# Weight block sums made in the units that use them, first-half operands prepared on a plan, three raw tiles for the second half's operands

## The chip, the cores and the metric

The kernel runs on one core of a Trainium2 chip. The metric is the device time of one execution in microseconds (us), lower is better. A profiled execution gives the trace; the other executions are timed without the profiler. The engines of a core are TensorE (PE: matmul, and PEld: its weight load), VectorE (DVE), ScalarE (ACT), GpSimd (POOL) and SyncE (SP), which here only issues DMAs. Each engine works through its own instructions in a fixed order.

## What is computed

One layer of a streaming encoder over 2048 frames of width 1024, in float32: a mixer of four groups, projected back and added to the input, and then a feed-forward network (FFN). The change touches the end of the mixer's output projection and the FFN:

```python
y = rmsnorm(y, group_norm[l].reshape(N_GROUPS, GROUP_W)).reshape(bsz, seq, D_MIX)
x = x + (y @ w_out[l]).astype(x.dtype)
h = rmsnorm(x, norm_ffn[l])
x = x + (jnp.square(jax.nn.relu(h @ w_ff1[l])) @ w_ff2[l]).astype(x.dtype)
```

`w_ff1` is 1024 x 4096, `w_ff2` is 4096 x 1024.

## The kernel before

**Precision.** Each float32 operand is split into a high part (ScalarE copies it to a rounded type, hi) and a low part (VectorE subtracts, lo = x - hi), and each product runs as three matmuls, hi·hi, hi·lo and lo·hi.

**The FFN products** are done in Winograd's form of Strassen's scheme: 2 x 2 blocks, seven block products in place of eight, with sums of blocks before and after. The time axis is cut in two halves `hf`, each of two blocks of 512 frames.

**Output projection.** `outp(b)` for the four blocks b of 512 frames: two column halves, four tiles each, 24 matmuls a tile (L510 to L512 in the trace); the result and the residual x are added (L1101) in a tile with tag `xr` and stored in `x1_d[b]`. `outp` yields 32 times, every 6 matmuls. `out_in(b)` makes the operand of the projection, in `hh` and `hl`, from the stored group outputs. `out_in(b + 1)` runs beside the second half of `outp(b)`; `dense(g, side)` lets the main generator `g` run, advances `side` at given steps, and `advance()` steps the generators that `track` has registered. After the loop over b = 0, 1, 2 the mixer's pools are closed, and `outp(3)` runs.

**Operands of the first FFN product.** `prep_step(hf, i, put, tmp)` takes 128 rows of the two time blocks of a half from `x1_d` (L1234, tiles with tag `xt`, two buffers), norms them (L1236 to L1238, gain in a tile with tag `gain`), transposes them on PE (L1228) and forms the seven operands, of which `put` splits each (L1267, L1268). Operands 5 and 6 lie in the buffers `hh` and `hl`, which the output projection reads until its last tile. For the first half the four steps are written behind `outp(3)` with a high priority; for the second half they run inside the first product at j = 2, 5, 8, 11, and the seven operands are kept in DRAM (`tb_d`). `from_dram` (L1286 to L1288) loads these in 14 pieces of 512 KB through the two `xt` buffers when the second half begins, and splits them.

**First product.** For each half and each j of 16, `w_units(j)` loads four blocks of `w_ff1` into the ring of raw tiles (tag `wr`, six buffers, L1204), forms four sums (L1208; two of them in tiles with tag `xr`, `tmpw`) and splits seven operands (L1198, L1199; nine buffers each of `wh`, `wl`). `ff1` then does seven products of 12 matmuls (`prod`, L1324), squares the ReLU (L1330, L1331), and stores seven operands for the second product in `as_d`.

**Second product.** Seven passes n, in the order AT = (0, 1, 6, 2, 3, 4, 5) of the block products; eight tiles q in each; 48 matmuls a tile (L1489). The tile of `as_d` is loaded through the two `xt` buffers and split (`s_tile`, L1457 to L1459). The weight operand of pass n and block row k is made by `t_unit(n, k)`: a raw tile of `w_ff2`, or of the sums in DRAM `tt_d`, split into one of 23 pairs of buffers (9 of `wh`/`wl`, 14 of `vh`/`vl`). The units of pass n + 1 are written in pass n, from q = 3 on, with a high priority.

**Sums for the second product.** `w2_step(n)`, 32 of them, loads pieces of the four blocks of a block row of `w_ff2` into one of two tiles named `w2r` (L1419), makes four sums with VectorE (L1208, 128 x 256) and stores them in `tt_d` (L1434). They are written into the second product's loop; the order that the framework's scheduler makes of it, which is fixed when the kernel is built, has them from within the first product on, wherever their buffers allow.

The framework sets the order of instructions on each engine, by priority and by when buffers come free; SyncE's DMA issues have such an order too, and an issue that waits holds up the ones behind it.

Of the kernel before, what the change touches and what calls it, by code (L numbers as in the profile page):

```python
# [21 lines left out]
P = 128  # L22
# [37 lines left out]
def emit(ctx, tc, a):  # L60
# [994 lines left out]
                yield  # L1055


    def out_in(b):
        yh, yl = hh, hl
        ya = c1.tile([P, 2, TB], F32, tag="gain", name="yat")  # L1060
        SY.dma_start(out=ya, in_=ya_d[b].rearrange("(c p) t -> p c t", p=P))

        def load(i):
            yt = big.tile([P, 3 * GW], F32, tag="xt", name="ybt", bufs=2)
            r0 = (b % 2) * TB + i * P
            SY.dma_start(out=yt[:, 0:GW], in_=yb_d[b // 2][r0:r0 + P, :])
            SY.dma_start(out=yt[:, GW:], in_=ycd_d[b][i * P:(i + 1) * P, :])
            return yt

        nx = load(0)  # L1070
        yield
        for i in range(4):
            ti = slice(i * P, (i + 1) * P)
            yt = nx
            if i < 3:
                nx = load(i + 1)
            S.activation(out=yh[:, 0:2, ti], in_=ya[:, :, ti], func=AF.Copy)
            V.tensor_tensor(out=yl[:, 0:2, ti], in0=ya[:, :, ti], in1=yh[:, 0:2, ti], op=ALU.subtract)
            for k3 in range(2):
                pt = psum_tr()  # L1080
                for k in range(3):
                    kk = k3 * 3 + k
                    PE.transpose(pt[:, k * P:(k + 1) * P], yt[:, kk * P:(kk + 1) * P], ident)
                pv = pt[:, 0:384].rearrange("p (k t) -> p k t", k=3)
                oh = yh[:, 2 + k3 * 3:5 + k3 * 3, ti]
                ol = yl[:, 2 + k3 * 3:5 + k3 * 3, ti]
                S.activation(out=oh, in_=pv, func=AF.Copy)
                V.tensor_tensor(out=ol, in0=pv, in1=oh, op=ALU.subtract)
                yield
# [80 lines left out]
    for b in range(3):  # L1170
        g = outp(b)
        for n in range(16):
            next(g)
            advance()
        drain(*((), ("s5",), ("hg",))[b])
        nxt = out_in(b + 1)
        next(nxt)
        dense(g, nxt)
        run(nxt)
    mixs.close()  # L1180


# [1 line left out]

    NJ = DFF // (2 * P)
    as_d = [[dram.tile([P, 4, NJ, P], F32, name=f"as{i}_{h}") for h in range(2)] for i in range(7)]
    tt_d = [dram.tile([NJ, P, D], F32, name=f"tt{i}") for i in range(2)]
    tb_d = [dram.tile([P, 4, TB], F32, name=f"tb{i}") for i in range(7)]
    run(outp(3))

    f2 = ExitStack()
    th = f2.enter_context(tc.tile_pool(name="th", bufs=1, reuse_waits="tile"))
    hi_ = tc.high_priority
# [17 lines left out]
    def operands():  # L1211
        ops = []
        for i in range(5):
            ops.append([th.tile([P, 4, TB], F32R, tag=f"t{i}{p_}", name="tb") for p_ in "hl"])
        for n_ in ("hh", "hl"):
            both = big.tile([P, KD, TB], F32R, tag=n_, name="tb2")
            ops.append([both[:, 0:4], both[:, 4:8]])
        return ops

    g_ffn = c1.tile([P, D], F32, tag="gain", name="g_ffn")  # L1220
    with hi_():
        SY.dma_start(out=g_ffn, in_=a["norm_ffn"].partition_broadcast(P))

    def prep_step(hf, i, put, tmp):
        def trans(ps, xs, half):
            for k in range(4):
                kk = half * 4 + k
                PE.transpose(ps[:, k * P:(k + 1) * P], xs[:, kk * P:(kk + 1) * P], ident)  # L1228

        o = i * P  # L1230
        xs = []
        for tb in range(2):
            x_ = big.tile([P, D], F32, tag="xt", name="fxs", bufs=2)
            SY.dma_start(out=x_, in_=x1_d[hf * 2 + tb][o:o + P, :])  # L1234
            ss = c1.tile([P, 1], F32, tag="fss", name="fss", bufs=2)
            S.activation(out=junk, in_=x_, func=AF.Square, accum_out=ss)  # L1236
            r = rstd_of(c1, ss, 1, 1.0 / D, "frs")
            V.scalar_tensor_tensor(out=x_, in0=x_, scalar=r, in1=g_ffn, op0=ALU.mult, op1=ALU.mult)  # L1238
            xs.append(x_)
        p11, p22 = psum_tr(), psum_sx()  # L1240
        trans(p11, xs[0], 0)
        trans(p22, xs[1], 1)
        s11, s22 = tmp(), tmp()
        S.activation(out=s11, in_=p11, func=AF.Copy)
        S.activation(out=s22, in_=p22, func=AF.Copy)
        p12, p21 = psum_tr(), psum_sx()
        trans(p12, xs[1], 0)
        trans(p21, xs[0], 1)
# [30 lines left out]

    def from_dram():  # L1280
        ops = operands()
        for i in range(7):
            for h in range(2):
                ks = slice(h * 2, h * 2 + 2)
                r = big.tile([P, 2, TB], F32, tag="xt", name="tr", bufs=2)
                SY.dma_start(out=r, in_=tb_d[i][:, ks, :])  # L1286
                S.activation(out=ops[i][0][:, ks], in_=r, func=AF.Copy)  # L1287
                V.tensor_tensor(out=ops[i][1][:, ks], in0=r, in1=ops[i][0][:, ks], op=ALU.subtract)  # L1288
        return ops
# [2 lines left out]
        return a["w_ff2"][(2 * k + half) * P:(2 * k + half + 1) * P, nd * 512:(nd + 1) * 512]  # L1292


    def w_units(j, tmp):
        f0 = j * 2 * P

        def raw(kh, fh):
            return raw512(a["w_ff1"][kh * 512:(kh + 1) * 512, f0 + fh * P:f0 + (fh + 1) * P]
                          .rearrange("(k p) c -> p k c", p=P))  # L1300

        with hi_():
            a11, a12, a21, a22 = raw(0, 0), raw(1, 0), raw(0, 1), raw(1, 1)
            u = [split(a11), split(a12)]
            s1, s2 = tmpw(), tmpw()
# [66 lines left out]
    def tmpw():  # L1372
        return c1.tile([P, 512], F32, tag="xr", name="tw", bufs=2)

    with hi_():
        b = operands()
        for i in range(4):
            prep_step(0, i, put_split(b), tmp1)
    nxt = w_units(0, tmp1)
    for hf in range(2):  # L1380
        for j in range(NJ):
            u = nxt
# [14 lines left out]
        return t2p.tile([P, 512], F32, tag="tq", name="tq", bufs=NT2)  # L1397

    units = [0]
    NB2 = 14  # L1400

    def split2(raw):
        n = units[0] % (NW + NB2)
        units[0] += 1
        return split(raw) if n < NW else split(raw, t2p, ("vh", "vl"), NB2)

    w2s = {}  # L1410

    def w2_load(n):
        k, c = n // 2, n % 2
        if n % 2:
            t_ = c1.tile([P, 4, 256], F32, tag="gain", name="w2r")
        else:
            t_ = t2p.tile([P, 4, 256], F32, tag="w2r", name="w2r")
        for h in range(2):
            SY.dma_start(out=t_[:, 2 * h:2 * h + 2, :], in_=a["w_ff2"][(2 * k + h) * P:(2 * k + h + 1) * P, :]  # L1419
                         .rearrange("p (d c) -> p d c", d=2)[:, :, c * 256:(c + 1) * 256])  # L1420
        w2s[n] = t_

    def w2_step(n):
        k, c = n // 2, n % 2
        if n + 1 < 2 * NJ:
            w2_load(n + 1)
        t_ = w2s.pop(n)
        b11, b12, b21, b22 = (t_[:, i, :] for i in range(4))
        tsub(b11, b12, b11)
        tsub(b12, b22, b12)  # L1430
        tsub(b22, b22, b11)
        tsub(b21, b21, b22)
        for h in range(2):
            SY.dma_start(out=tt_d[h][k].rearrange("p (d c) -> p d c", d=2)[:, :, c * 256:(c + 1) * 256],  # L1434
                         in_=t_[:, 2 * h:2 * h + 2, :])
# [4 lines left out]
    def t_unit(n, k):  # L1440
        i = AT[n]
        with hi_():
            if i in (0, 1, 6):
                return split2(raw512(w2(k, *((0, 0), (1, 0), None, None, None, None, (1, 1))[i])))
            h, c = ((1, 1), (0, 1), (1, 0), (0, 0))[i - 2]
            return split2(raw512(tt_d[h][k][:, c * 512:(c + 1) * 512]))

    scnt = [0]

# [23 lines left out]

    tu = {(0, k): t_unit(0, k) for k in range(NJ)}
    s_next = s_tile(0, 0)
    w2_load(0)
    done = 0
    for n in range(7):
        for q in range(8):
            st_ = s_next  # L1480
# [6 lines left out]
            for k in range(NJ):  # L1487
                for p_, (ls, lt) in enumerate(PASS):
                    PE.matmul(ps, lhsT=st_[:, ls, k, :], rhs=tu[n, k][lt], start=k == 0 and p_ == 0,  # L1489
                              stop=k == NJ - 1 and p_ == 2)  # L1490
                while k in (3, 11) and done < min(2 * NJ, (34 * (8 * n + q) + 17 * (k == 11)) // 18):
                    w2_step(done)
                    done += 1
            if n == 0:
                S.activation(out=X[:, q], in_=ps, func=AF.Copy)
            elif n == 1:
# [40 lines left out]
```

## Time and profile before

| What | us |
|---|---|
| median of three timed runs (2323.58, 2324.29, 2330.36) | 2324.29 |
| the profiled execution, its own time | 2333.46 |
| its span, first to last instruction | 2331.7 |
| last matmul of the output projection starts (L511 row) | 1006.9 |
| first product's matmuls (L1324), first and last start | 1007.4 and 1680.4 |
| second product's matmuls (L1489), first and last start | 1680.6 and 2326.2 |

The table divides the span: mixer and projection fill the first 1007 us, the first FFN product the next 673, the second the last 646. How the time in a stage is read: the count of matmuls in a window against its width tells whether PE is full, since a matmul's recorded duration overlaps the next one's. In a row of a window, "(x110)" is the count; in a row of waits stand the total in us, the number of waits and the longest; in a row of a group or a line, min, median and max in ns, and when the first and last one start.

### The profile page before, as it was taken

Reading aid. Unit: us, or ns where it says so; the run is one execution under the profiler, and the core shown is the slowest. Engines: PE = TensorE matmul, PEld = TensorE weight load, DVE = VectorE, ACT = ScalarE, POOL = GpSimd, SP = SyncE. Lnnn points to the kernel's source line nnn. Section 1 sums busy time; section 2 is a strip of 40 time slices with the busy share of each in tenths; the row PEclk is TensorE's granted clock in tenths of the full one; section 3 lists DMA queues with packets and bytes.
Section 4 is the critical chain, followed back from the end, with each engine's and each line's share of the span. In section 5 each row is a group of like instructions: output and inputs, shape, how many; then the busy total and the mean of one; then the engine's idle time right before and its main releaser. Section 6 shows DMA issues by size and latency. Waiting matters only on the chain. (4 is left out here: it accounts for less than half of the span.)

```text
span 2331.7 us, 32589 instructions
## 1 busy us (share of the span) xinstructions
PE 2222.9 (95%) x11460; PEld 1759.5 (75%) x11460; DVE 1444.6 (62%) x3080; ACT 957.8 (41%) x1902; POOL 185.2 (8%) x235
## 2 busy tenths in 40 slices
PE   4999999999999999999999999999999989999999
PEld 3767777777777777777787767788877767888887
DVE  4796796796689654686666676655544445344343
ACT  3343425325433432455554565555533133233121
POOL 3112212112211110000000000000000000000000
PEclk9999999999999999999999999999999999999999
DMA  6323344443543466645677788555567666354454
GB/s 171 99 83 93 97 106 126 116 113 91 147 112 95 147 202 220 216 139 168 190 215 237 217 271 247 163 149 149 171 222 230 217 221 198 100 174 143 165 172 149
DMA packets 412900, 381.36 MB, mean 164 GB/s; under 512 B 31088, under 2 KB 338384, under 8 KB 412736
## 3 DMA queue, kind: packets, MB, share of 16 engines
q1 hardware_dynamic: 411680, 377.63, 52.8%
q0 software_dynamic: 1056, 1.64, 0.6%
q8 instruction: 90, 1.47, 0.3%
q14 instruction: 74, 0.61, 0.1%
HBM read 261.77 MB, written 116.40 MB: 162 GB/s over the span
## 5 line engine op out<-in xcount | busy, mean ns | idle before, releaser
L1489 PE MATMUL mm<-wh,st 128*128 128x512 f32 x1792 | 565.4, 396 | 15.2 <-DVE st L1459 7.1
L1489 PEld LDWEIGHTS mm<-wh,st 128*128 128x128 f32 x1792 | 337.1, 189 | 100.1 <-DVE st L1459 12.3
L1489 PE MATMUL mm<-wl,st 128*128 128x512 f32 x896 | 354.2, 395 | 0.0
L1324 PE MATMUL mm<-tb,wh 128*128 128x512 f32 x1024 | 329.5, 403 | 20.5 <-ACT tp L1343 9.7
L1458 ACT ACTIVATE st<-sr 128x1024 fp32r<-128x1024 f32 x112 | 116.0, 1056 | 411.3 <-PE mm L1489 247.5
L1324 PEld LDWEIGHTS mm<-tb,wh 128*128 128x128 f32 x1024 | 193.1, 192 | 75.7 <-ACT tp L1343 15.8
L510 PE MATMUL mm<-wh,hh 128*128 128x512 f32 x512 | 213.0, 416 | 0.7 <-ACT hh L505 0.7
L105 ACT ACTIVATE wh<-wr 128x512 fp32r<-128x512 f32 x224 | 139.0, 629 | 170.5 <-PE mm L511 113.7
L512 PE MATMUL mm<-wh,hl 128*128 128x512 f32 x512 | 205.7, 402 | 0.0
L511 PE MATMUL mm<-wl,hh 128*128 128x512 f32 x512 | 204.9, 400 | 0.0
L1324 PE MATMUL mm<-tb,wl 128*128 128x512 f32 x512 | 203.8, 401 | 0.0
L1489 PEld LDWEIGHTS mm<-wl,st 128*128 128x128 f32 x896 | 168.9, 189 | 40.2 <-DVE wl L1199 0.6
L1198 ACT ACTIVATE wh<-wr 128x512 fp32r<-128x512 f32 x208 | 125.9, 625 | 122.7 <-PE mm L1324 71.5
L111 DVE TENSOR_TENSOR wl<-wr,wh 128x512 fp32r<-128x512 f32 x224 | 151.2, 692 | 35.1 <-ACT wh L105 33.7
L1324 PE MATMUL hx<-tb,wh 128*128 128x512 f32 x512 | 162.7, 396 | 5.1 <-ACT tb L1287 2.0
L1459 DVE TENSOR_TENSOR st<-sr,st 128x1024 fp32r<-128x1024 f32 x112 | 133.9, 1221 | 49.9 <-ACT st L1458 49.4
L510 PE MATMUL mm<-hh,wh 128*128 128x512 f32 x384 | 159.4, 415 | 0.0
L1199 DVE TENSOR_TENSOR wl<-wr,wh 128x512 fp32r<-128x512 f32 x208 | 138.1, 685 | 28.8 <-ACT wh L1198 28.4
L512 PE MATMUL mm<-hh,wl 128*128 128x512 f32 x384 | 152.8, 398 | 0.0
L511 PE MATMUL mm<-hl,wh 128*128 128x512 f32 x384 | 152.5, 397 | 0.0
L1208 DVE TENSOR_TENSOR w2r<-w2r 128x256 f32<-128x256 f32 x128 | 54.1, 423 | 136.9 <-DMA w2r<-in_w_ff_dram 129.5
L1324 PEld LDWEIGHTS hx<-tb,wh 128*128 128x128 f32 x512 | 96.1, 188 | 30.4 <-ACT wh L1198 3.0
(395 smaller groups left out, 3599.8 us busy)
## 6 DMA issues: line engine op xcount, KB each, us to landing
as<-tp SPq DMA_DIRECT2D x224, 256.0 KB, 2.8
sr<-as SPq DMA_DIRECT2D x112, 512.0 KB, 4.5
wr<-in_w_ff_dram SPq DMA_DIRECT2D x176, 256.0 KB, 3.8
wr<-in_w_in_dram SPq DMA_DIRECT2D x160, 256.0 KB, 3.1
wr<-in_w_out_dram SPq DMA_DIRECT2D x64, 256.0 KB, 4.0
w2r<-in_w_ff_dram SPq DMA_DIRECT2D x64, 256.0 KB, 4.2
tt<-w2r SPq DMA_DIRECT2D x64, 256.0 KB, 3.6
wr<-tt SPq DMA_DIRECT2D x64, 256.0 KB, 4.0
```

Of the source, the lines that this page charges most:

```text
L105: S.activation(out=hi, in_=raw, func=AF.Copy)
L111: (G if le == "p" else V).tensor_tensor(out=lo, in0=raw, in1=hi, op=ALU.subtract)
L510: PE.matmul(ps, lhsT=lh, rhs=rh, start=first, stop=False)
L511: PE.matmul(ps, lhsT=lh, rhs=rl, start=False, stop=False)
L512: PE.matmul(ps, lhsT=ll, rhs=rh, start=False, stop=last)
L1198: S.activation(out=h, in_=raw, func=AF.Copy)
L1199: V.tensor_tensor(out=l, in0=raw, in1=h, op=ALU.subtract)
L1208: V.tensor_tensor(out=o, in0=x, in1=y, op=op)
L1324: PE.matmul(ps, lhsT=(wh, wl)[lw][:, ks], rhs=b[lb][:, k, :], start=first and k == 0 and q == 0, stop=k == 3 and q == 2, skip_group_check= ...
L1458: S.activation(out=s_[:, 0, ks], in_=r, func=AF.Copy)
L1459: V.tensor_tensor(out=s_[:, 1, ks], in0=r, in1=s_[:, 0, ks], op=ALU.subtract)
L1489: PE.matmul(ps, lhsT=st_[:, ls, k, :], rhs=tu[n, k][lt], start=k == 0 and p_ == 0, stop=k == NJ - 1 and p_ == 2)
```

## The change

Three parts.

- `w2_step`, `w2_load` and the tiles `w2r` go. `t_unit` loads the raw blocks of `w_ff2` into the ring and makes the sums there, on VectorE, before it splits: three blocks and two sums for block product 2, whose result GpSimd stores in `tt_d` for product 4; two blocks and one sum for products 3, 4 and 5. The buffers for split units grow from 23 pairs to 26 (15 of `vh`/`vl`, one of the two `xr` tiles, one in the `gain` tile).
- The loop over b ends with the first half of `outp(2)`; the FFN's pools are opened there. `out_in(3)` takes its two blocks of group A in two temporary tiles. `prep_step` is divided into loads (`prep_load`), a first (`prep_a`) and a second part (`prep_b`), and a generator `preps` does the four steps of the first half at fixed steps of the plan beside the rest of `outp(2)` and `outp(3)`; steps 0 and 2 load half rows into temporary tiles. Operands 5 and 6 are held in temporaries until `outp(3)` has ended. `w_units(0)` is written ahead of the last eight steps of `outp(3)`, with its sums in temporary tiles.
- `from_dram` takes every third piece through the `gain` tile.

```diff
-    def out_in(b):
+    def out_in(b, ya_t=None):
         yh, yl = hh, hl
-        ya = c1.tile([P, 2, TB], F32, tag="gain", name="yat")
-        SY.dma_start(out=ya, in_=ya_d[b].rearrange("(c p) t -> p c t", p=P))
+        if ya_t is None:
+            yv = c1.tile([P, 2, TB], F32, tag="gain", name="yat")
+            SY.dma_start(out=yv, in_=ya_d[b].rearrange("(c p) t -> p c t", p=P))
+        else:
+            ya = [ya_t(), ya_t()]
+            for c in range(2):
+                SY.dma_start(out=ya[c], in_=ya_d[b][c * P:(c + 1) * P, :])
...
         drain(*((), ("s5",), ("hg",))[b])
-        nxt = out_in(b + 1)
-        next(nxt)
-        dense(g, nxt)
-        run(nxt)
+        if b < 2:
+            nxt = out_in(b + 1)
+            next(nxt)
+            dense(g, nxt)
+            run(nxt)
     mixs.close()
...
-    run(outp(3))
...
+    def prep_load(hf, i, tmp=None):
...
+            if tmp is None:
+                x_ = big.tile([P, D], F32, tag="xt", name="fxs", bufs=2)
+                SY.dma_start(out=x_, in_=src)
+                halves = [x_[:, 0:512], x_[:, 512:]]
+                parts = [(x_, g_ffn)]
+            else:
+                halves = [tmp(), tmp()]
+                for n, x_ in enumerate(halves):
+                    SY.dma_start(out=x_, in_=src[:, n * 512:(n + 1) * 512])
+                parts = [(x_, g_ffn[:, n * 512:(n + 1) * 512]) for n, x_ in enumerate(halves)]
+            ss = c1.tile([P, 2], F32, tag="fss", name="fss", bufs=2)
+            for n, (x_, g_) in enumerate(parts):
+                S.activation(out=junk[:, 0:x_.shape[1]], in_=x_, func=AF.Square, accum_out=ss[:, n:n + 1])
+            if len(parts) == 2:
+                V.tensor_tensor(out=ss[:, 0:1], in0=ss[:, 0:1], in1=ss[:, 1:2], op=ALU.add)
...
     def from_dram():
         ops = operands()
+        last_operands(ops)
         for i in range(7):
             for h in range(2):
                 ks = slice(h * 2, h * 2 + 2)
-                r = big.tile([P, 2, TB], F32, tag="xt", name="tr", bufs=2)
+                if (2 * i + h) % 3 == 2:
+                    r = c1.tile([P, 2, TB], F32, tag="gain", name="tr")
+                else:
+                    r = big.tile([P, 2, TB], F32, tag="xt", name="tr", bufs=2)
...
+    def put_or_hold(i, o, src):
+        if i < 5:
+            split_now(i, o, src)
+        else:
+            held.append((i, o, src))
+    def preps():
+        xs, ab = {}, {}
+        plan = {0: "L0", 9: "A0", 11: "B0", 12: "L1", 14: "L2", 22: "A1", 24: "B1", 25: "L3", 28: "A2", 30: "B2",
+                36: "A3", 38: "B3"}
...
+    nxt = out_in(3, tmp1)
+    next(nxt)
+    track(preps(), 1.0, "pp")
+    dense(g, nxt)
+    run(nxt)
+    g = outp(3)
+    for n in range(24):
+        next(g)
+        advance()
+    nxt = w_units(0, tmp1, tmp1)
+    dense(g)
+    drain("pp")
+    last_operands(b)
     with hi_():
-        b = operands()
-        for i in range(4):
-            prep_step(0, i, put_split(b), tmp1)
-    nxt = w_units(0, tmp1)
+        for i, o, src in held:
+            split_now(i, o, src)
...
-    def w2_load(n):
...
-    def w2_step(n):
...
-            h, c = ((1, 1), (0, 1), (1, 0), (0, 0))[i - 2]
-            return split2(raw512(tt_d[h][k][:, c * 512:(c + 1) * 512]))
+            r = raw512(w2(k, *((1, 1), (1, 1), (1, 0), (0, 1))[i - 2]))
+            x = raw512(tt_d[k] if i == 4 else w2(k, *((0, 1), (0, 1), None, (0, 0))[i - 2]))
+            tsub(r, r, x)
+            if i == 2:
+                tsub(r, r, raw512(w2(k, 0, 0)), ALU.add)
+                G.dma_start(out=tt_d[k], in_=r)
+            return split2(r)
```

More of the change, by code (lines that the diff above doesn't have):

```diff
@@ L1076, in out_in @@
                 nx = load(i + 1)
-            S.activation(out=yh[:, 0:2, ti], in_=ya[:, :, ti], func=AF.Copy)
-            V.tensor_tensor(out=yl[:, 0:2, ti], in0=ya[:, :, ti], in1=yh[:, 0:2, ti], op=ALU.subtract)
+            if ya_t is None:
+                S.activation(out=yh[:, 0:2, ti], in_=yv[:, :, ti], func=AF.Copy)
+                V.tensor_tensor(out=yl[:, 0:2, ti], in0=yv[:, :, ti], in1=yh[:, 0:2, ti], op=ALU.subtract)
+            else:
+                for c in range(2):
+                    S.activation(out=yh[:, c, ti], in_=ya[c][:, ti], func=AF.Copy)
+                    V.tensor_tensor(out=yl[:, c, ti], in0=ya[c][:, ti], in1=yh[:, c, ti], op=ALU.subtract)
             for k3 in range(2):
@@ L1186, in emit @@
     as_d = [[dram.tile([P, 4, NJ, P], F32, name=f"as{i}_{h}") for h in range(2)] for i in range(7)]
-    tt_d = [dram.tile([NJ, P, D], F32, name=f"tt{i}") for i in range(2)]
+    tt_d = dram.tile([NJ, P, 512], F32, name="tt")
     tb_d = [dram.tile([P, 4, TB], F32, name=f"tb{i}") for i in range(7)]
-    run(outp(3))
     f2 = ExitStack()
@@ L1214, in operands, with last_operands @@
             ops.append([th.tile([P, 4, TB], F32R, tag=f"t{i}{p_}", name="tb") for p_ in "hl"])
+        return ops
+    def last_operands(ops):
         for n_ in ("hh", "hl"):
@@ L1217, in operands @@
             ops.append([both[:, 0:4], both[:, 4:8]])
-        return ops
     g_ffn = c1.tile([P, D], F32, tag="gain", name="g_ffn")
@@ L1222, in emit @@
         SY.dma_start(out=g_ffn, in_=a["norm_ffn"].partition_broadcast(P))
[L1224 to L1228, printed above, removed]
+    def prep_load(hf, i, tmp=None):
         o = i * P
@@ L1232, in prep_step, with prep_trans, prep_a @@
         for tb in range(2):
[L1233 to L1239, printed above, removed]
+            src = x1_d[hf * 2 + tb][o:o + P, :]
+            if tmp is None:
[13 more added lines that the diff above has]
+                V.tensor_tensor(out=ss[:, 0:1], in0=ss[:, 0:1], in1=ss[:, 1:2], op=ALU.add)
+            r = rstd_of(c1, ss[:, 0:1], 1, 1.0 / D, "frs")
+            for x_, g_ in parts:
+                V.scalar_tensor_tensor(out=x_, in0=x_, scalar=r, in1=g_, op0=ALU.mult, op1=ALU.mult)
+            xs.append(halves)
+        return xs
+    def prep_trans(ps, x_):
+        for k in range(4):
+            PE.transpose(ps[:, k * P:(k + 1) * P], x_[:, k * P:(k + 1) * P], ident)
+    def prep_a(xs, tmp):
         p11, p22 = psum_tr(), psum_sx()
-        trans(p11, xs[0], 0)
-        trans(p22, xs[1], 1)
+        prep_trans(p11, xs[0][0])
+        prep_trans(p22, xs[1][1])
         s11, s22 = tmp(), tmp()
@@ L1245, in prep_step, with prep_b @@
         S.activation(out=s22, in_=p22, func=AF.Copy)
+        return s11, s22
+    def prep_b(i, xs, s11, s22, put, tmp):
+        o = i * P
         p12, p21 = psum_tr(), psum_sx()
-        trans(p12, xs[1], 0)
-        trans(p21, xs[0], 1)
+        prep_trans(p12, xs[1][0])
+        prep_trans(p21, xs[0][1])
         put(0, o, s11)
@@ L1262, in prep_step @@
         put(6, o, t4)
+    def prep_step(hf, i, put, tmp):
+        xs = prep_load(hf, i)
+        prep_b(i, xs, *prep_a(xs, tmp), put, tmp)
     def put_split(ops):
@@ L1292, in w2, with w_units @@
         return a["w_ff2"][(2 * k + half) * P:(2 * k + half + 1) * P, nd * 512:(nd + 1) * 512]
-    def w_units(j, tmp):
+    def w_units(j, tmp, tw=None):
         f0 = j * 2 * P
@@ L1304, in w_units @@
             u = [split(a11), split(a12)]
-            s1, s2 = tmpw(), tmpw()
+            s1, s2 = (tw or tmpw)(), (tw or tmpw)()
             tsub(s1, a21, a22, ALU.add)
@@ L1373, in tmpw @@
         return c1.tile([P, 512], F32, tag="xr", name="tw", bufs=2)
+    b, held = operands(), []
+    split_now = put_split(b)
+    def put_or_hold(i, o, src):
+        if i < 5:
+            split_now(i, o, src)
+        else:
+            held.append((i, o, src))
[3 more added lines that the diff above has]
+                36: "A3", 38: "B3"}
+        for n in range(39):
+            what, i = plan.get(n, "--")
+            if what == "L":
+                xs[i] = prep_load(0, int(i), tmp1 if i in "02" else None)
+            elif what == "A":
+                ab[i] = prep_a(xs[i], tmp1)
+            elif what == "B":
+                prep_b(int(i), xs.pop(i), *ab.pop(i), put_or_hold, tmp1)
+            yield
+    nxt = out_in(3, tmp1)
[11 more added lines that the diff above has]
+    last_operands(b)
     with hi_():
-        b = operands()
-        for i in range(4):
-            prep_step(0, i, put_split(b), tmp1)
-    nxt = w_units(0, tmp1)
+        for i, o, src in held:
+            split_now(i, o, src)
     for hf in range(2):
@@ L1399, in emit @@
     units = [0]
-    NB2 = 14
+    NB2 = 15
     def split2(raw):
-        n = units[0] % (NW + NB2)
+        n = units[0] % (NW + NB2 + 2)
         units[0] += 1
-        return split(raw) if n < NW else split(raw, t2p, ("vh", "vl"), NB2)
-    w2s = {}
-    def w2_load(n):
[L1413 to L1421, printed above, removed]
-    def w2_step(n):
[L1424 to L1435, printed above, removed]
+        if n < NW:
+            return split(raw)
+        if n < NW + NB2:
+            return split(raw, t2p, ("vh", "vl"), NB2)
+        if n == NW + NB2:
+            return split(raw, c1, ("xr", "xr"), 2)
+        both = c1.tile([P, 2, 512], F32R, tag="gain", name="wg")
+        S.activation(out=both[:, 0], in_=raw, func=AF.Copy)
+        V.tensor_tensor(out=both[:, 1], in0=raw, in1=both[:, 0], op=ALU.subtract)
+        return both[:, 0], both[:, 1]
     AT = (0, 1, 6, 2, 3, 4, 5)
@@ L1475, in emit @@
     s_next = s_tile(0, 0)
-    w2_load(0)
-    done = 0
     for n in range(7):
@@ L1490, in emit @@
                               stop=k == NJ - 1 and p_ == 2)
-                while k in (3, 11) and done < min(2 * NJ, (34 * (8 * n + q) + 17 * (k == 11)) // 18):
-                    w2_step(done)
-                    done += 1
             if n == 0:
```

## The prediction

> **What bounds the kernel now.** I read the page's header first, then the table of windows for the FFN, then the waits.
>
> ```profile
> span 2331.7 us, 32589 instructions
> PE 2222.9 (95%) x11460; PEld 1759.5 (75%) x11460; DVE 1444.6 (62%) x3080; ACT 957.8 (41%) x1902; POOL 185.2 (8%) x235
> ```
>
> PE bounds the kernel, so only PE time that is not filled can be won. The change touches nothing before the second half of the third output projection, about 920 us; the rest I cut where the first FFN product (L1324) and the second (L1489) run. Columns: window, its width, PE busy with (count of matmuls), weight loads, clock, DMA share, GB/s.
>
> ```profile
> 1007.40:1040.00 32.60, 29.13 (x110) 21.78 (x110) 0.90 0.35 104
> 1040.00:1200.00 160.00, 151.11 (x632) 118.30 (x631) 0.99 0.66 194
> 1200.00:1330.00 130.00, 119.92 (x495) 94.09 (x495) 0.97 0.74 223
> 1330.00:1400.00 70.00, 64.91 (x272) 50.12 (x271) 1.00 0.86 261
> 1400.00:1480.00 80.00, 76.76 (x320) 60.20 (x320) 0.98 0.74 222
> 1480.00:1680.00 200.00, 200.00 (x864) 161.88 (x863) 1.00 0.52 152
> ...
> 1680.60:1710.00 29.40, 26.39 (x112) 20.59 (x112) 1.00 0.90 288
> 1710.00:1780.00 70.00, 70.00 (x304) 56.65 (x303) 1.00 0.60 188
> 1780.00:1940.00 160.00, 147.76 (x610) 115.31 (x609) 0.98 0.68 223
> 1940.00:2326.00 386.00, 386.00 (x1667) 312.57 (x1666) 1.00 0.48 158
> ```
>
> The window from 1480 is undisturbed: 200/864 = 0.2315 us a matmul. At that price the count says what each window lost: 7.1 us in 1007 to 1040 (32.6 - 110 x 0.2315), 13.7 + 15.4 + 7.0 + 5.9 in the next four, 3.5, nothing, 18.8 and nothing. Transposes have to come off. The next rows are those of L1228 alone, then all PE work and the matmuls into mm in the last projection.
>
> ```profile
> 1200.00:1330.00 130.00, 2.07 (x16) 1.87 (x16) 0.97 0.74 223
> ...
> 920.00:1007.00 87.00, 79.35 (x371) 63.06 (x370) 55.60 (x91) 40.37 (x73) 4.39 (x8) 0.96 0.62 201
> ...
> 920.00:1007.00 87.00, 71.62 (x283) 53.17 (x282) 7.76 (x12) 0.00 (x0) 0.96 0.62 201
> ```
>
> 16 transposes fill 2.07 us, 0.13 each. So 1040 to 1200, with the 48 of three steps, lost 13.7 - 6.2 = 7.5 us, 1200 to 1330 lost 15.4 - 2.1 = 13.3, and 920 to 1007 lost 87 - 283 x 0.2315 - 88 x 0.13 = 10.1. **All that can be won** is 10.1 + 7.1 + 7.5 + 13.3 + 7.0 + 5.9 + 3.5 + 18.8 = 73 us.
>
> Where the weight sums (w2_step) run is the next table, of the instructions on the tile w2r alone (VectorE busy and count).
>
> ```profile
> 1200.00:1330.00 130.00, 13.53 (x32) 0.97 0.74 223
> ...
> 1400.00:1480.00 80.00, 8.03 (x19) 0.98 0.74 222
> 1480.00:1680.00 200.00, 0.00 (x0) 1.00 0.52 152
> ...
> 1710.00:1780.00 70.00, 7.62 (x18) 1.00 0.60 188
> 1780.00:1940.00 160.00, 17.80 (x42) 0.98 0.68 223
> ...
> L1208 DVE TENSOR_TENSOR w2r<-w2r x128: 410/424/428, 1213.1 to 1939.1; 128x256 f32<-128x256 f32 x128
> ```
>
> PE loses time nearly where these run (the last row: 1213 to 1939), and none in the 586 us of the FFN from 1480 and from 1940 without them, though the FFN's own work is the same. The exception, 1710 to 1780, is free of loss with 18. The waits of 1200 to 1480 (VectorE), 1200 to 1340 (ScalarE, PE), and VectorE and SP around one tile at 1900, show how:
>
> ```profile
> DVE w2r L1208 <- DMA w2r<-in_w_ff_dram: 30.4, 15, 4.6
> DVE tw L1208 <- DMA wr<-in_w_ff_dram: 28.5, 12, 4.2
> ...
> ACT tp L1330 <- DVE tp L1208: 29.5, 17, 4.9
> ...
> PE mm L1324 <- ACT tp L1343: 7.8, 5, 2.5
> ...
> 1909.44 0.42 DVE L1208 TENSOR_TENSOR w2r<-w2r 128x256 f32<-128x256 f32 x1 [9.65 <-DMA w2r<-in_w_ff_dram]
> ...
> 1899.63 0.57 SPq L1434 DMA_DIRECT2D tt<-w2r  x1
> ...
> 1905.69 1.25 SPq L1419 DMA_DIRECT2D w2r<-in_w_ff_dram  x2
> 1911.03 1.46 SPq L1457 DMA_DIRECT2D sr<-as  x2
> ```
>
> A sum stands in VectorE's queue and waits for its load, the load waits for an older store to free its buffer, ScalarE's evictions wait for VectorE, PE for ScalarE. In the second product SP also holds the sr loads behind that chain.
>
> **The change, part by part.** *Sums leave the first product.* 128 subtractions of 0.424 us, 54 us in all, go, with their 64 loads and 64 stores; the 64 reads of tt become 16. The rows for what comes in their place:
>
> ```profile
> wr<-in_w_ff_dram SPq DMA_DIRECT2D x34, 256.0 KB, 5.1
> sr<-as SPq DMA_DIRECT2D x112, 512.0 KB, 4.5
> wgr<-in_s_w_glu_dram POOLq DMA_DIRECT2D x2, 256.0 KB, 3.9
> L1208 DVE TENSOR_TENSOR tw<-wr x32: 681/693/694, 1003.9 to 1631.0; 128x512 f32<-128x512 f32 x32
> ```
>
> The new units cannot move that early: their split buffers are held by older units until the second product. So 1200 to 1330 and 1400 to 1480 should look like 1480 to 1680. I take 12 of 13.3 and 5.5 of 5.9 us; the low ends, 6 and 3, leave half to the tw waits on raw weights, which stay.
>
> *The second product.* Its 18.8 us go, and a unit now does its own sums: 5 of 128x512 per k (2 + 1 + 1 + 1), 80 x 0.69 = 55 us on VectorE, as much as before, over four passes of 8 x 48 x 0.2315 = 88.9 us. The heaviest is n = 2, which builds the three-term units: 48 raw loads and 16 stores of 0.262 MB and 16 sr loads of 0.524 MB, 25.2 MB or 283 GB/s. The trace has had more, so the engines can carry it, barely:
>
> ```profile
> 1690.00:1700.00 10.00, 8.30 (x36) 6.46 (x36) 3.62 (x8) 1.65 (x4) 0.00 (x0) 1.00 0.98 327
> ```
>
> The ring of six raw tiles: the first tile of such a unit is held 5.1 (load) + 2 x 0.69 + 3.9 (store, by the POOL row) = 10.4 us, the others 5.8 and 6.5, 22.7 in all, 3.8 us a unit over six buffers, 61 us for 16 units. That fits. But with 26 split buffers only ten units can be ready early; the last six start as the last tile of the pass frees theirs, 6 x 3.8 = 23 us against 11.1 + 15 x 0.69 = 21.5 until the last is needed: 1.5 us late. The two-load units need about 2 us each and fit. The added wait is the subtraction at VectorE for the second and third raw tile; behind it stand splits of st and evictions, and PE waits for those after a tile's slack. Bounds: nothing lost, or 1.9 us in each of 32 tiles, 61 us (the last rival). I take 11 us (6 in n = 2, 5 in the other three), the nearest row being the loss-free 1940 on, which has units of one load at the same places. Gain 18.8 - 11 = 8 us. Start of the product, 3.5 us: unchanged, within 3 either way.
>
> *Three raw tiles in from_dram.* Half-operand loads and their splits:
>
> ```profile
> L1287 ACT ACTIVATE tb<-tr x14: 1043/1058/1063, 1339.2 to 1388.6; 128x1024 fp32r<-128x1024 f32 x14
> L1288 DVE TENSOR_TENSOR tb<-tr,tb x14: 1217/1224/1227, 1341.2 to 1389.9; 128x1024 fp32r<-128x1024 f32 x14
> ...
> DMA to landing us min/median/max: 4.6/5.1/6.1
> ```
>
> A buffer turns round in 5.1 + 1.06 + 1.22 = 7.4 us; 14 / 2 x 7.4 = 52 us, which is the 50 us between the first and the last split. With three, 14 / 3 x 7.4 = 34. PE lost 7.0 us there; 4 of it go (bounds 0 and 7).
>
> *Operands of the first half on a plan, w_units(0) without the xr tiles.* PE's longest wait in 920 to 1007:
>
> ```profile
> PE tr L1228 <- DVE fxs L1238: 4.6, 4, 2.5
> ```
>
> The transposes already run inside the last projection, so none of the 64 is saved; they only come 9 to 14 steps (6 matmuls, 6 x 0.2315 = 1.4 us each) after their loads, so this wait goes; out_in's own, the rest, stays. SP takes 12 loads of x1d in place of eight, and earlier, among the residual's loads, and two of the steps load in halves, with a sum more on VectorE and a read more on ScalarE; out_in(3) splits its first two blocks in eight pieces for four, at most 4 x 0.69 us more on each engine, under matmuls. That pays some back. I take 5 of 10.1 us (from 5 worse to 10 better). At the first product's start VectorE and ScalarE have only the held operands 5 and 6 to split, which PE needs 14 us in: 5 of 7.1 (0 to 7).
>
> **Sum:** 12 + 5.5 + 8 + 4 + 5 + 5 = 39.5, say 40 us. The profiled execution took 2333.5 us (span 2331.7), so it becomes 2293.5; the median of the three timed runs was 2324.3, 9.2 lower, and becomes **2284**.
>
> *A rule that speaks against it.* The stores of n = 2 are issued by GpSimd. VectorE is then busy 16 x (3 x 0.69 + 1.22) + 8 x 0.69 = 58 of 88.9 us, and before has no GpSimd DMA in the FFN. The Trainium skill (SBUF — State Buffer, "SBUF: two separate sides") warns that GpSimd cannot write DMA descriptors while VectorE runs an operation that takes both ports. By that rule read broadly the first rival below comes about; by its wording, which names VectorE's two-port modes, and with sums that take 0.69 us for 512 columns, it does not. No run here shows either yet.
>
> **The rivals.**
> *Stores held back* by a busy VectorE: each first tile is kept some 3 us more (four sums and splits of 0.69), 16 x 3 / 6 = 8 us over n = 2 if nothing hides it: 2292. For: the issue engine is new there. Against: a slack of 28 us in the pass.
> *The first product's losses are its own*, VectorE's tw waits for raw weights (28.5 us), not the w2r's: the 17.5 us stay, 2284 + 17.5 = 2302. Against: 1480 to 1680.
> *Half the harm*: new waits like 1780 to 1940, 18.8 us over 14.4 tiles, 1.3 a tile in 32 tiles, 42 us against 11: 2284 + 31 = 2315.
> *Nothing lost in the four passes and a smooth projection*: 2284 - 11 - 5 = 2268 or a little less.
> *Slower*: one mechanism, VectorE's fixed order in the second product. The chain of waits has two tiles in a row that were paced by load and store:
>
> ```profile
> 1910.92 1.22 DVE st L1459
> ...
> 1923.98 1.22 DVE st L1459
> ```
>
> They stand 13.06 us apart, 11.1 undisturbed. If two units a tile with two or three loads pace all 32 tiles so, 1.9 us each, that is 61 us, less the 18.8 that go and the 31.5 won elsewhere: 10 us slower, 2335. It decides from (31.5 + 18.8) / 32 = 1.6 us a tile. Against it: a third of VectorE's time is free, the ring is deeper (six against two), and loads do not wait for stores except through one tile in three.
>
> **How the numbers follow.** The forecast, 2284, has 0.58 (its own bounds 2268 to 2300); stores held back 0.08; first product's own losses 0.12; half the harm 0.08; the smooth case 0.06; slower 0.08. The range leaves out the slower case and the far half of "half the harm": 2260 to 2314. About 0.3%, 7 us, is what a measurement of this kernel can tell from no change: 2317 divides faster from same. Half the harm lies next to that border, so a quarter of it counts as faster: faster 0.86, same 0.06, slower 0.08.
>
> **What would show it.** Right: no w2r; L1324's windows from 1200 on as full as 864 in 200 us except at the from_dram loads; tr splits within 35 us; L1228 with no wait. Wrong: VectorE idle before L1208 for wr in the second product with PE waiting for st (more than 1.6 us a tile is the slower case); SP standing at L1204 with sr behind it; first product windows as thin as now.

## The result and the profile after

The median after is 2294.54 us (four runs, 2291.91 to 2304.97) against 2324.22 for before: a ratio of 0.9863, 95% interval 0.9838 to 0.9889, or 29.7 us less. The profiled execution took 2296.33 us, 37.1 less than before's. First the header of the page.

```profile
span 2294.5 us, 32511 instructions
...
PE 2205.3 (96%) x11460; PEld 1755.9 (77%) x11460; DVE 1449.5 (63%) x3044; ACT 961.3 (42%) x1914; POOL 194.4 (8%) x251
```

There are as many matmuls as before, and VectorE is as busy as before. Of the 37.2 us that the span lost, 17.6 are busy time of PE (2222.9 to 2205.3) and 19.6 its idle time: a matmul's record is longer where the granted clock is low (0.63 us in place of 0.39 in the pass n = 5 below). So the share of busy time doesn't tell what was won, and the count of matmuls does. Next the first product, cut at about the places of the prediction's table (matmuls of L1363, formerly L1324, with their count; weight loads; granted clock; DMA share; GB/s).

```profile
1007.00:1040.00 33.00, 31.39 (x132) 24.50 (x132) 1.00 0.40 118
1040.00:1200.00 160.00, 155.54 (x659) 122.23 (x658) 1.00 0.66 196
1200.00:1310.00 110.00, 108.63 (x466) 86.70 (x465) 1.00 0.63 183
1310.00:1380.00 70.00, 67.70 (x283) 53.48 (x282) 0.98 0.75 225
1380.00:1450.00 70.00, 70.00 (x302) 56.21 (x302) 1.00 0.54 158
1450.00:1648.00 198.00, 197.97 (x854) 159.96 (x852) 1.00 0.53 153
```

At 0.2315 us a matmul the third row is full: 466 x 0.2315 = 107.9, and 16 transposes at 0.13 make 110.0. Most of what is left stands in the fourth row, where the second half's operands are loaded: 70 - 283 x 0.2315 = 4.5 us. The first two rows, with 8 and 40 transposes, keep 1.4 and 2.2. Their splits now lie within 34 us, in place of 50:

```profile
L1326 ACT ACTIVATE tb<-tr x14: 1042/1058/1065, 1314.8 to 1348.7; 128x1024 fp32r<-128x1024 f32 x14
```

In the second product the first pass, n = 0, keeps about the loss that it had (4.1 us, 3.4 in before), and two more of the seven passes are not full (matmuls of L1548; a pass has 384, or 88.9 us, and two more reach into the window):

```profile
2103.00:2200.70 97.70, 91.62 (x386) 73.93 (x385) 0.97 0.63 203
1829.60:1924.00 94.40, 91.06 (x386) 71.67 (x385) 1.00 0.78 261
```

These are n = 5, with 8.8 us lost, and n = 2, with 5.5. The second was forecast; the first was not, and is one wait. VectorE and SP around it, from the timeline (start, duration, engine, line, tile; in brackets the idle time before and what ended it):

```profile
2133.50 0.69 DVE L1217 TENSOR_TENSOR wr<-wr 128x512 f32<-128x512 f32 x1 [1.19 <-DMA wr<-in_w_ff_dram]
2134.11 1.22 DVE L1520 TENSOR_TENSOR st<-sr,st 128x1024 fp32r<-128x1024 f32 x1
2138.46 0.69 DVE L1217 TENSOR_TENSOR wr<-wr 128x512 f32<-128x512 f32 x1 [3.13 <-DMA wr<-in_w_ff_dram]
2140.96 0.69 DVE L1217 TENSOR_TENSOR tq<-tq,X 128x512 f32<-128x512 f32 x1 [1.81 <-DMA tq<-x1d]
2141.68 0.69 DVE L1217 TENSOR_TENSOR tq<-mm,tq 128x512 f32<-128x512 f32 x1
```

```profile
2128.84 2.69 SPq L1213 DMA_DIRECT2D wr<-in_w_ff_dram  x2
...
2134.22 0.33 SPq L1213 DMA_DIRECT2D wr<-in_w_ff_dram  x1
2135.36 0.32 SPq L1518 DMA_DIRECT2D sr<-as  x1
2135.73 0.42 SPq L1529 DMA_DIRECT2D tq<-x1d  x1
```

`finish` adds the residual `x1d` to a result before it evicts the bank (`tq<-mm,tq`). SP issues that load only at 2135.73, behind raw loads that wait for the ring and a load of `sr` that waits for a split. VectorE stands first for a raw tile, 3.13 us, and then 1.81 us for this load, which ends its wait at 2140.96; the bank comes free after 2141.68. PE, which needs the bank, pays twice:

```profile
2136.00:2142.00 6.00, 0.45 (x2) 0.01 (x1) 0.92 0.88 299
2142.00:2148.00 6.00, 5.48 (x13) 4.40 (x14) 0.51 0.64 202
```

In 6 us 26 matmuls can start. One does in the first window (the other in its count began earlier), so 25 are missing, or 5.8 us; 13 are missing in the second, where PE runs, but at a granted clock of 0.51, or 3.0 us. Together that is the 8.8 us of the pass. Why n = 5 alone: it is the only pass in which the three conditions meet, residual loads for `finish`, units of two loads in the making (those of n = 6), and both in SP's one order. Pass 1 has `finish` with units of one load; pass 6 makes no units.

**Loss by stage.** The table adds up, from one matmul's start to the next, what exceeds 0.2315 us (0.13 after a transpose, where a shorter step counts as no loss), in us of each kernel's profiled execution. FFN stretches count from the first matmul of the first product; "sums" are 193 to 303 and 393 to 473 together, where before ran its w2r chain, "operands" 303 to 393, where the second half's are loaded.

| kernel | projection from 815 | start, 0 to 33 | 33 to 193 | sums | operands | n = 1 and 2 | n = 5 |
|---|---|---|---|---|---|---|---|
| before | 16.5 | 7.2 | 9.2 | 16.4 | 11.4 | 19.7 | 0.5 |
| before, again | 12.7 | 7.5 | 4.4 | 11.1 | 12.3 | 18.0 | 0.5 |
| after | 17.0 | 1.7 | 4.0 | 1.2 | 5.1 | 5.3 | 8.8 |
| after, again | 15.1 | 1.5 | 3.6 | 1.0 | 7.6 | 2.1 | 9.6 |
| after, third | 15.0 | 1.7 | 4.1 | 2.2 | 4.3 | 4.6 | 10.0 |
| before without sums | 14.5 | 6.9 | 5.4 | 1.8 | 5.5 | 0.4 | 0.5 |
| sums only | 13.2 | 6.7 | 4.6 | 1.4 | 6.7 | 5.1 | 9.9 |
| plan and third raw tile only | 13.3 | 1.2 | 2.2 | 7.1 | 6.5 | 17.8 | 0.5 |
| units without sums | 15.3 | 1.6 | 2.7 | 1.4 | 5.6 | 0.4 | 0 |
| sum's store on SP | 11.3 | 1.7 | 3.5 | 1.4 | 5.5 | 0.4 | 9.8 |
| output's loads on GpSimd | 14.7 | 1.5 | 3.3 | 1.8 | 4.6 | 3.4 | 0 |
| residual loads too | 20.2 | 1.2 | 4.3 | 1.6 | 6.1 | 7.2 | 0 |
| both moves | 13.9 | 1.6 | 3.0 | 1.6 | 4.4 | 0.4 | 0 |

Not in the table: pass 0 keeps 3.3 to 7.5 us in every kernel, and the first product from 473 on loses 0.3 or 0.4, but 3.7 with the plan and third raw tile only. The first columns differ between profiles of one kernel by up to 5 us, so only larger steps, or steps that return in several rows, are read from this table.

### The profile page after: what moved, and what is told of

Read it like the earlier page. It is cut to its first block, busy times and chain, and to the rows that moved or that the text cites. A ratio compares the mean times of both kernels' runs of the same rounds, so it can differ in the third digit from the quotient of the medians.

```text
span 2294.5 us, 32511 instructions
## 1 busy us (share of the span) xinstructions
PE 2205.3 (96%) x11460; PEld 1755.9 (77%) x11460; DVE 1449.5 (63%) x3044; ACT 961.3 (42%) x1914; POOL 194.4 (8%) x251
## 4 chain that ended last, share of the span: by engine, by line
PE 42%; DMA 6%; DVE 3%; ACT 1%; issue 1%; SPq 0%; DVEq 0%; ACTq 0%
PE mm L1548 19%; PE mm L1363 13%; PE hx L1363 7%; DMA wr<-in_w_ff_dram 5%; PE mx L1363 3%; DVE st L1520 1%; DMA tr<-tb 1%; DMA sr<-as 1%; DVE wr L1217 1%; DVE wl L1208 0%; ACT wh L1207 0%; ACT st L1519 0%; DMA tq<-x1d 0%; DVE tp L1217 0%; DVE tb L1327 0%
## 5 line engine op out<-in xcount | busy, mean ns | idle before, releaser
L1548 PE MATMUL mm<-wh,st 128*128 128x512 f32 x1728 | 549.2, 395 | 13.8 <-DVE tq L1217 6.1
L1548 PEld LDWEIGHTS mm<-wh,st 128*128 128x128 f32 x1728 | 325.8, 189 | 92.3 <-issue 9.6
L1548 PE MATMUL mm<-wl,st 128*128 128x512 f32 x864 | 341.1, 395 | 0.2 <-DVE wl L1208 0.2
L1363 PE MATMUL mm<-tb,wh 128*128 128x512 f32 x1024 | 323.8, 397 | 4.0 <-ACT tp L1369 1.9
L1363 PEld LDWEIGHTS mm<-tb,wh 128*128 128x128 f32 x1024 | 190.9, 189 | 53.7 <-ACT tp L1382 5.4
L1363 PE MATMUL mm<-tb,wl 128*128 128x512 f32 x512 | 202.4, 396 | 1.0 <-DVE wl L1208 1.0
L1548 PEld LDWEIGHTS mm<-wl,st 128*128 128x128 f32 x864 | 162.8, 188 | 38.9 <-DVE wl L1208 0.9
L1363 PE MATMUL hx<-tb,wh 128*128 128x512 f32 x512 | 161.1, 394 | 0.0
L1363 PEld LDWEIGHTS mm<-tb,wl 128*128 128x128 f32 x512 | 96.6, 189 | 23.7 <-DVE wl L1208 1.4
L510 PEld LDWEIGHTS mm<-wh,hh 128*128 128x128 f32 x512 | 98.6, 193 | 20.8 <-ACT hh L505 1.3
```

The lines of the kernel that those rows point to most:

```text
L510: PE.matmul(ps, lhsT=lh, rhs=rh, start=first, stop=False)
L1363: PE.matmul(ps, lhsT=(wh, wl)[lw][:, ks], rhs=b[lb][:, k, :], start=first and k == 0 and q == 0, stop=k == 3 and q == 2, skip_group_check= ...
```

## The experiments

**The same two kernels again**, for the spread. No edit.

> The kernel before once more, for a second profile. If the 9.2 us between its profiled execution (2333.5) and its median (2324.3) belong to the profiler, which lengthens its chains of store and load, this profiled execution is again at 2330 to 2336. If they were chance, it is at 2322 to 2328, with fewer lost matmuls in 920 to 1040 or 1780 to 1940.

> The changed kernel once more, for a closer interval and a second profile. The prediction's sum went by the profiled execution and by an offset of 9.2 us to the median. If the 6.1 us wait of PE at 2142 us (pass n = 5, VectorE at the output tile tq) comes from the fixed order of VectorE and SP, it stands in the second profile within 2 us of its size; if it was chance, the second product is 6 to 9 us shorter and the profiled execution near 2288. Median expected 2292 to 2295 either way.

Before's second profiled execution took 2319.1 us, 14.4 less than its first. After: 2292.12 us (six runs, 2286.86 to 2299.42), ratio 0.9866 (0.9837 to 0.9895); the wait in n = 5 is there again. So the 9.2 us by which before's first profile stood over the median belonged to that execution, not to profiling.

**The sums alone, and everything but the sums.** The first is before with `t_unit` and `split2` of the change; the second is after with those of before:

```diff
-            h, c = ((1, 1), (0, 1), (1, 0), (0, 0))[i - 2]
-            return split2(raw512(tt_d[h][k][:, c * 512:(c + 1) * 512]))
+            r = raw512(w2(k, *((1, 1), (1, 1), (1, 0), (0, 1))[i - 2]))
+            x = raw512(tt_d[k] if i == 4 else w2(k, *((0, 1), (0, 1), None, (0, 0))[i - 2]))
+            tsub(r, r, x)
...
-                while k in (3, 11) and done < min(2 * NJ, (34 * (8 * n + q) + 17 * (k == 11)) // 18):
-                    w2_step(done)
-                    done += 1
```

> The kernel before with the first part of the change alone: sums in the units that use them, 26 pairs of split buffers; first half's operands and from_dram as before. Theory that the sums' chain was what held PE: 12 + 5.5 us come back in the first product and about 8 in the second, 2324 - 25 = 2299, and the first product's windows after the first 30 us are full but for the steps of the second half and from_dram. Rival, that the gain is the plan's and the early weight units': 2315 or more.

> The change without its first part: w2_step, its two tiles and 23 pairs of buffers as before; plan, early weight units and three raw tiles as changed. Theory that the sums' chain held PE: 5 us at the first product's start and up to 4 at from_dram, nothing in the projection, 2324 - 8 = 2316. Rival, that plan and early units pay: 2300 or less.

Sums only: 2302.24 us, 0.9907 (0.9882 to 0.9931). Plan and third raw tile only: 2310.73, 0.9946 (0.9926 to 0.9966). Before's median beside them was 2320.49, so the first won 18.3 us of the 25 that were expected, and the second 9.8, a little more than the expected 8. The two reductions, 0.0093 and 0.0054, add up to 0.0147, near the 0.0137 of the whole. In the table each part keeps to its own columns: "start" follows the plan, "sums" and n = 1 and 2 follow the sums. Where the second kernel keeps its chain, that chain's first sum starts at 1358.6 in place of 1213.1, and "sums" falls from 11 to 16 down to 7 with no sum gone, only moved, and part of the loss moved along: this is the kernel that loses 3.7 us behind 473.

```profile
L1217 DVE TENSOR_TENSOR w2r<-w2r x128: 412/425/428, 1358.6 to 1911.7; 128x256 f32<-128x256 f32 x128
```

**Before without its chain.** Nothing is loaded into w2r, summed or stored; the units of block products 2 to 5 load raw blocks, so the sums are missing from the computation.

```diff
-            h, c = ((1, 1), (0, 1), (1, 0), (0, 0))[i - 2]
-            return split2(raw512(tt_d[h][k][:, c * 512:(c + 1) * 512]))
+            return split2(raw512(w2(k, *((1, 1), (0, 1), (1, 0), (0, 0))[i - 2])))
...
-                while k in (3, 11) and done < min(2 * NJ, (34 * (8 * n + q) + 17 * (k == 11)) // 18):
-                    w2_step(done)
-                    done += 1
```

> The kernel before without its chain of weight sums: nothing is loaded into w2r, summed or stored, and the units of block products 2 to 5 load raw blocks, so the sums are missing from the computation. Theory (the chain makes before's thin windows): the stretches 193 to 303 and 393 to 473 us into the first product lose 1 to 2 us in place of 10 and 6, n=1 and n=2 under 1 us each in place of 7 to 8 and 11, and 303 to 393 keeps 7 us, the turnround of two raw tiles; about 30 to 35 us less, 2288 to 2293. Rival (the first product's losses are its own, VectorE's waits for raw weights): these two stretches keep 12 us or more, and the time stays above 2300.

2292.67 us (2287.09 to 2296.36), 0.9849 (0.9831 to 0.9867): the chain cost 35 us. Its windows (L1324, and in the last row L1486 over pass 2), and the splits of the second half's operands:

```profile
1203.00:1313.00 110.00, 107.97 (x463) 86.13 (x462) 1.00 0.63 182
1313.00:1403.00 90.00, 87.21 (x367) 67.64 (x366) 1.00 0.70 211
1403.00:1483.00 80.00, 80.00 (x347) 64.53 (x346) 1.00 0.52 152
```

```profile
1842.20:1931.80 89.60, 89.60 (x385) 72.09 (x385) 1.00 0.46 147
```

```profile
L1287 ACT ACTIVATE tb<-tr x14: 1043/1059/1062, 1325.4 to 1371.4; 128x1024 fp32r<-128x1024 f32 x14
```

All three places fill up with nothing else touched, so the chain made them thin. The run takes out the chain's transfers together with its work on VectorE and SP, and doesn't divide the 35 us between them; that a high rate alone doesn't thin a pass is seen further down (both moves: 271 GB/s in pass 2, 0.6 us lost). VectorE's waits for raw weights, the rival, stay nearly as long as they were (1203 to 1483; 28.5 us in before), and PE hardly feels them:

```profile
DVE tw L1208 <- DMA wr<-in_w_ff_dram: 25.4, 13, 3.0
```

The kernel shows one more thing: with two raw tiles the splits take 46 us, and "operands" loses 5.5, no more than after with three (4.3 to 7.6). Of the 11 to 12 us lost there before, the chain's part was about 6; the third raw tile made the loads quicker, and that alone saves PE nothing that these profiles show.

**After without the sums**: the same question from the other side. Each unit loads one raw block; the subtractions, the other loads and the stores are left out.

```diff
-            x = raw512(tt_d[k] if i == 4 else w2(k, *((0, 1), (0, 1), None, (0, 0))[i - 2]))
-            tsub(r, r, x)
-            if i == 2:
-                tsub(r, r, raw512(w2(k, 0, 0)), ALU.add)
-                G.dma_start(out=tt_d[k], in_=r)
```

> The changed kernel with the sums left out: t_unit loads one raw block for block products 2 to 5, with no subtraction, no second load and no store of tt_d, so outputs are not the reference's. It prices what the units' own sums cost PE. Theory that they cost PE about 11 us (5 to 6 in pass n = 2, 9 in n = 5, by the profiles of the changed kernel): both passes lose under 1 us and the median falls by 11 to 15 us, to 2278 to 2281. Rival, that these waits belong to the output tiles and the split of st and would be there anyway: under 4 us.

2280.24 us (2272.48 to 2285.22), 0.9809 (0.9789 to 0.983). Against the changed kernel's 0.9863 that is 12.5 us (0.0054 of 2322), the price of the sums where they now stand; against its two other measurements, 0.9866 and 0.9847 below, it is 13.2 and 8.8. Pass 2 loses 0.6, at 146 GB/s where after moves 261 (the window shown holds all but its last 5 us), and pass 5 loses nothing:

```profile
1829.00:1918.00 89.00, 89.00 (x384) 71.77 (x383) 34.43 (x42) 25.32 (x32) 0.00 (x0) 1.00 0.45 146
```

(Columns as on the page: PE, PEld, DVE, ACT and POOL with their counts.)

**The sum's store on SP.**

```diff
-                G.dma_start(out=tt_d[k], in_=r)
+                SY.dma_start(out=tt_d[k], in_=r)
```

> The changed kernel with the store of tt_d issued by SyncE in place of GpSimd. Rival of the prediction, that GpSimd's stores are held back by a busy VectorE: pass n = 2 gets shorter, its loss of 2 to 6 us goes. Theory that they are not: n = 2 is the same or longer by 2 to 8 us, since SyncE's loads now stand behind a store that waits for VectorE's sum. Median 2292 to 2300 against 2284 to 2288 by the rival.

2289.38 us (2285.74 to 2293.85), 0.9853 (0.9835 to 0.987): pass 2 loses 0.6 in place of 2.3 to 5.5, pass 5 still 9.8. In pass 2 the rival's sign came, not that of the expectation's theory; by the time nothing is shown, as the interval overlaps that of the changed kernel.

**The output's residual loads on GpSimd, and the projection's too.**

```diff
         r = tmp2()
-        SY.dma_start(out=r, in_=x1_d[b_][t0:t0 + P, nd * 512:(nd + 1) * 512])
+        G.dma_start(out=r, in_=x1_d[b_][t0:t0 + P, nd * 512:(nd + 1) * 512])
...
-                SY.dma_start(out=xr, in_=a["x"][t0:t0 + P, ns])
+                G.dma_start(out=xr, in_=a["x"][t0:t0 + P, ns])
```

> The changed kernel with the load of x1d into the output tile (finish) issued by GpSimd, all else as changed. Theory for the wait of 6 to 7 us at the third tile of pass n = 5: the load stands in SyncE's order behind raw loads that wait for ring buffers, so VectorE's output sum and PE's PSUM buffer wait with it. Then n = 5 loses under 3 us in place of 9, median 2285 to 2288. Rival, that VectorE stands at its own sums for raw tiles and the load is no part of it: n = 5 loses 7 to 10 us still, median 2291 to 2294.

> As the kernel before in this list, and the loads of x in outp issued by GpSimd too. Theory that the projection's loss (13 to 17 us from 815 us on, the same with and without the plan) is VectorE standing at the residual sum for a load that SyncE issued late, behind weight loads: PE's waits for hl at 885, 935 and 967 us go, and 5 to 8 us with them, median 2278 to 2282. Rival, that the load's own time or VectorE's load sets it: within 2 us of the kernel without.

The first hunk alone: 2289.62 us (2283.88 to 2295.63), 0.9851 (0.9832 to 0.987). The wait in n = 5 is gone. Pass 3, which had 0 to 1, lost 4.0 in this profile, on one wait for an eviction, so the profile gives back near half; the other profiles with this edit have 5.5 and 0.6 there, and why isn't settled. Pass 0 may give back more: it loses 5.8 to 7.5 in the three kernels with this edit, where PE stands 2.1 to 4.6 us for one eviction of ScalarE (L1551), against 3.3 to 4.1 in the other kernels with the plan. But sums only (6.5) and before without its chain (5.9) reach as much without the edit, so it isn't shown to be the cause.

```profile
PE mm L1548 <- DVE Y L1217: 3.0, 1, 3.0
```

With the second hunk: 2296.76 (2288.53 to 2304.26), 0.9885 (0.9866 to 0.9903), and the projection loses 20.2, no less than before. The expectation failed. The loads on GpSimd stand and wait for something else:

```profile
889.04 1.15 POOL L1109 DMA_DIRECT2D xr<-in_x_dram  x2 [9.78 <-DMA x1d<-xr]
```

The load needs one of two `xr` tiles, and a tile comes free when its store to `x1d` has landed. At its longest waits it is that loop of two tiles, not the queue of the load, that the load stands for.

**Both moves**, the store on SP and the output's loads on GpSimd, beside the changed kernel on the same chip.

> The changed kernel with both moves that took a wait out of the second product: the three-term sums are stored by SyncE, and the residual of the output is loaded by GpSimd. Theory (the two waits are separate: pass n=2 waits for raw buffers that the store keeps, pass n=5 for residual loads held up on SyncE): n=2 loses under 1 us in place of 2 to 5, n=5 none in place of 9, the other passes as in the changed kernel; 9 to 12 us less than the changed kernel's 2292 to 2295, so 2280 to 2285. Rival (what is taken out of n=5 comes back at n=0 and n=3, as in the run with the output's loads alone on GpSimd, because the wait is VectorE's fixed order and only its place moves): n=0 and n=3 lose 3 us each more, 2287 to 2290, no better than either move alone.

> The changed kernel on the same chip as the run with both moves, so that the two are compared directly: 2290 to 2296. If the spread of its times covers the other kernel's, the step of 9 to 12 us isn't shown.

Both moves: 2286.95 us (five runs, 2282.05 to 2289.22), 0.983 (0.9817 to 0.9844). After: 2291.58 (2289.06 to 2295.24), 0.9847 (0.9833 to 0.9862). The profile does what the theory said, 0.6 us in n = 2 and none in n = 5, and pass 3 stays at 0.6, while pass 0 loses 7.5:

```profile
1829.20:1918.70 89.50, 89.50 (x385) 72.12 (x384) 1.00 0.82 271
2097.50:2186.40 88.90, 88.90 (x385) 72.11 (x384) 1.00 0.68 220
```

The time does half of it: 4.6 us between the medians, where 9 to 12 were expected, with the two intervals still touching, and 2286.95 lies between the theory's 2280 to 2285 and the rival's 2287 to 2290. That it beats the changed kernel is likely, not shown; that it beats either move alone (0.9853 and 0.9851) isn't shown either.

## Why the prediction was right, and where it was off

The sign and the range held, and the forecast, 2284, was 10 us too low. Its terms against the table (mean of before's two profiles less the mean of after's three):

| step of the prediction | forecast gain | measured |
|---|---|---|
| sums leave the first product ("sums") | 17.5 | 13.8 - 1.5 = 12.3 |
| from_dram ("operands") | 4 | 11.9 - 5.7 = 6.2 |
| start of the first product | 5 | 7.4 - 1.6 = 5.8 |
| 1040 to 1200 ("33 to 193") | 0 | 6.8 - 3.9 = 2.9 |
| second product (its whole length) | 8 | 645.3 - 639.7 = 5.6 |
| projection | 5 | 14.6 - 15.7 = -1.1 |
| sum | 39.5 | 31.7 |

The measured sum lies by the three differences of medians: 29.7, 28.4 and 36.2 us.

**The first product's mechanism was right.** The w2r chain thinned its windows, as before without its chain shows; "the first product's losses are its own" (2302) is refuted. The size was off, for a reason that lies in the working: the terms were read from an execution that stood 9.2 us above the median, and the whole of their sum was then taken from the median. In before's other profile "sums" holds 11.1 us, not 16.4, and "33 to 193" 4.4, not 9.2. An execution that is slower than the median has losses that the median doesn't have; a gain read from it is too large for the median. That is the step "2324.3, 9.2 lower, and becomes 2284": between the two profiled executions the time fell by 37.1, not far from the 39.5 of the sum. That the sum fits so well there is in part luck, since terms that gave less (projection, second product) and terms that gave more (operands, 33 to 193) cancel.

**from_dram's gain came for another reason than the one given.** The turnround was right: 52 to 34 us forecast, 50 to 34 measured. That PE gets its time from it was not: before without the chain has 46 us of loads and loses as little. That some gain came in this row is luck.

**The projection's 5 us failed.** The step said that PE's wait for `fxs` goes and that this is worth 5 of 10.1. The wait went, and one of the same length stands in its place, behind `out_in`'s splits (waits of PE after, 920 to 1007; the last row has its like in before, 2.3 us):

```profile
PE tr L1264 <- DVE hl L1098: 2.5, 1, 2.5
...
PE tr L1093 <- DVE hl L1098: 2.0, 1, 2.0
```

In the eight profiles with the plan (the projection's residual loads unaltered) "projection" lies between 11.3 and 17.0, mean 14.5; in the four without it between 12.7 and 16.5, mean 14.2. The plan is worth nothing there that can be seen. What sets this loss isn't settled; the one trial at it, moving its loads, made it no better.

**The second product.** What goes was sized right, 18.8 against 18.9. The new waits were forecast at 11, "6 in n = 2, 5 in the other three". They are 4.2 in n = 2, 9.0 more than before in n = 5, next to nothing in n = 3 and 4: 13.2 us by the profiles (means), and 9 to 13 by the times of after without the sums. It is near in sum by luck, and wrong in place: the prediction looked for PE behind `st` and behind evictions in general, and missed that SP's order also carries the loads of `finish`. *Slower*, 1.9 us in every tile, and *half the harm*, 1.3, did not come: 13.2 / 32 = 0.4.

*Stores held back* was priced at 8 us and 3 us a tile. The landing times (issues with count, size, median from issue to landing), after and then with both moves:

```profile
tt<-wr POOLq DMA_DIRECT2D x16, 256.0 KB, 4.5
```

```profile
tt<-wr SPq DMA_DIRECT2D x16, 256.0 KB, 4.1
```

These two lie 0.4 us apart; over all profiles the median is 4.4 to 5.0 from GpSimd and 3.8 and 4.1 from SP, so a store takes 0.3 to 1.2 us more, not 3. PE loses about 4 us to it in pass 2 in the profiles (0.6 in both kernels with the store on SP, against 2.3 to 5.5). So the issue engine has some part in pass 2, well under the rival's price; how so little a store becomes that, and how much of it is GpSimd's turn, isn't shown. The Trainium skill (SBUF — State Buffer, "SBUF: two separate sides") advises SyncE or ScalarE for such a DMA, as GpSimd cannot write descriptors while VectorE runs in a two-port mode. The trace agrees with the advice in its sign, and doesn't show a lockout.

## What to carry to other kernels

Where an engine that works in a fixed order stands at a load that waits for a store, look for the price at the engine that it feeds, and try it by leaving the chain out whole: here a chain with 54 us of hidden VectorE work cost PE 35. Before moving such work, list everything else in the issuing queue's order: a load that was harmless (`finish`'s residual) became the one long wait. And take a gain off the profile only after a second profile of the same kernel; forecast the difference for an execution near the median.

## What the runs showed of the hardware

A wait of PE can cost more than its length. In before's pass 1, PE stands 1.89 us for an eviction (timeline), and from 1834 to 1838 it runs at a mean granted clock of 0.59 (windows of L1489):

```profile
1833.25 0.48 PE L1489 MATMUL mm<-wh,st 128*128 128x512 f32 x1 [1.89 <-DVE tq L1208]
```

```profile
1830.00:1834.00 4.00, 2.07 (x9) 1.09 (x7) 1.00 0.25 90
1834.00:1838.00 4.00, 3.71 (x10) 2.90 (x11) 0.59 0.84 238
```

By the starts of its matmuls PE loses 4.3 us here: 2.0 at the wait, 0.6 at two gaps right behind it, and 1.7 in ten matmuls that start 0.31 to 0.43 us apart in place of 0.23. The 6.1 us wait in after's pass 5 cost 8.8 in all. Not every wait does this: in before's second profile PE stands 3.12 us up to 1255.64, runs at a granted clock of 1.00 behind it (1256 to 1260), and loses little more than the wait. The Trainium skill (TensorE: Matmul & The Clock Gate, "What's actually happening") gives about 3.4 us as the idle window after which the clock halves; here it fell after a wait of 1.9 and not after one of 3.12, so the length of a single wait does not decide it in these traces, and what does isn't shown. One wait can so be worth more than its share in a list of waits, and the loss is better taken from the count of matmuls.
